# Weights' buffers at 96 instead of 64 bytes, modulo 512, above the activation slots

## Chip, cores and metric

One core of one Trainium2 chip runs the whole program. The metric is device time in microseconds (us) of one execution; lower is better. The engines are TensorE (PE, with its weight loads shown as PEld), VectorE (DVE), ScalarE (ACT), GpSimd (POOL) and the queue of SyncE (SP), which issues the transfers. SBUF is the on-chip memory, with 128 partitions; an address here is a byte offset within a partition, the same in all 128.

## What is computed

Two blocks of two transformer layers each, on 256 tokens of width 1024, in float32. Cut to its order:

```
x = first_block(x, mem, ...)     # layer 0: gated 31-wide causal convolution + memory attention
                                 # layer 1: forgetting attention + memory attention
                                 # each followed by a projection and a convolved FFN (2 x 2816 wide)
x = second_block(x, p, ...)      # retention (4 heads) + per-layer embedding,
                                 # sparse attention (16 heads; compressed, selected, window) + embedding
...
logits = einsum("bqhd,bkhd->bhqk", qb, kb) * scale + cum_logf[q] - cum_logf[k]
u = causal_dwconv(h @ w_up, w_dw, b_dw); gate, val = split(u, 2)
return (silu(gate) * val) @ w_down
```

Nearly all of the arithmetic is activations (1024 or 2816 by 256 tokens) times weight matrices, some 180 MB of weights read once.

## The kernel before

Activations are kept with channels on partitions and the 256 tokens along the partition. The weights stream from memory in one fixed order as units of 128 x 1024 float32 (512 KB), `ws[i]`, each with eight chunks of 128 x 128. `load` (SP) brings a unit into one of four `raw` buffers, some units ahead of use; `advance` (line 483 on) splits it: ACT rounds it to fp32r into `whi` (line 501), DVE or POOL subtracts to get the rest into `wlo` (line 505). There are six `whi` and six `wlo` buffers in turn. The early stages (to about 123 us: embeddings, gated convolution, memory keys) take their units unsplit, as plain float32 (`NATIVE`, tiles `wf`).

Activations that feed a split matmul lie in slots: 45 tiles of 128 x 512 fp32r, the first 256 columns the rounded half, `hi`, the others the rest, `lo` (`Split`). 38 slots are in the pool `const`; 7 more (`LATE`) are added in a pool of their own when the phase `ffn0` begins, behind a tile `gap` that nothing reads. A product of split operands is three matmuls, `mm3`, with the first argument as the stationary operand (the weight load) and the second as the moving one:

```python
    def mm3(ps, ahi, alo, bhi, blo, start, stop):
        pe.matmul(ps, lhsT=ahi, rhs=bhi, start=start, stop=False)
        pe.matmul(ps, lhsT=ahi, rhs=blo, start=False, stop=False)
        pe.matmul(ps, lhsT=alo, rhs=bhi, start=False, stop=stop)
```

These are lines 554 to 556. `proj` calls it with a weight chunk as the stationary operand and a slot's half as the moving one (one output tile of 128 channels by 256 tokens per eight or more chunks). `proj_tm` (lines 585 to 587) has the roles changed: a slot's 128 tokens are stationary, up to 512 columns of weights move. Attention logits and values have slots on both sides. Results go to PSUM tiles `acc`, `s`, `pt` or `o`, whose names stand ahead of the arrow in the rows; behind it stands the moving operand and then the stationary one. Line 572 is `proj` with unsplit weights. `conv31` (lines 859 to 868) applies 31 taps to a tile `vp` at starts that go up by one column (4 bytes): 5 taps on PE, 10 or 11 on ACT (line 865), the rest on DVE (line 868).

The order of the work on each engine is the program's own order, laid out by the tile framework, which also sets the waits. Each pool gets one stretch of a partition, in the order in which pools are opened: `const`, `wraw` (the `raw` tiles), `wspl` (`whi`, `wlo`, `wf`), `fp`, `tiny`, then the phase's pool, or from `ffn0` on the late slots and after them the phase's pool. Tiles begin at multiples of 32 bytes. In the program before, all slots, the late ones too, begin at 256 modulo 512; `raw`, `whi`, `wlo`, `wf` and the tiles of `fp` begin at 320 modulo 512. `epsc` (line 549) lies in `const` behind the slots and takes 32 bytes; the late pool's `gap` takes 64.

Of the kernel before, what the change touches and what calls it, by code (L numbers as in the profile page):

```python
# [18 lines left out]
F32 = mybir.dt.float32  # L19
# [5 lines left out]
P = 128  # L25
# [367 lines left out]
def block_kernel(ctx, tc, A, out, WL, PL, CL, SL, stop=None, dbg=None):  # L393
# [3 lines left out]
    const = ctx.enter_context(tc.tile_pool(name="const", bufs=1))  # L397
# [3 lines left out]
    tiny = ctx.enter_context(tc.tile_pool(name="tiny", bufs=4))  # L401
    dram = ctx.enter_context(tc.tile_pool(name="dram", bufs=1, space=bass.MemoryType.DRAM))
    psum = ctx.enter_context(tc.tile_pool(name="psum", bufs=1, space=bass.MemoryType.PSUM))

    rmk, r1k, rr, r3k = (const.tile([P, 2], F32, name=n) for n in ("rmk", "r1k", "rr", "r3k"))
    slots = Slots(const, NSLOTS - LATE)

# [28 lines left out]
    def phase(nm):  # L436

        phases.close()
        if nm == "ffn0":
            lp = late.enter_context(tc.tile_pool(name="late", bufs=1))  # L440
            lp.tile([P, 16], F32, name="gap")
            slots.add(lp, LATE)
        cur[0] = phases.enter_context(tc.tile_pool(name=nm, bufs=1))

# [101 lines left out]
    pool.memset(ones, 1.0)  # L546
    mhalf = const.tile([P, 2], F32, name="mhalf")
    pool.memset(mhalf, -0.5)
    epsc = const.tile([P, 2], F32, name="epsc")
    pool.memset(epsc, 1e-6)  # L550


# [137 lines left out]


    phase("conv")
    def token_stats(t, junk, ss, tt):

# [306 lines left out]

    def ffn(l, X, st, gains, stats):
        phase(f"ffn{l}")
        rb = None
        h = []
# [63 lines left out]
    def small(nm):  # L1069
# [6 lines left out]
        return hi, lo  # L1076

    phase("fox")
    wf = small("f")

# [766 lines left out]
```

## Time and profile before

| | |
|---|---|
| median of 3 runs | 1190.87 us (1187.84, 1190.87, 1197.31) |
| the profiled execution's own time | 1191.61 us |
| span of its profile, first to last instruction | 1189.8 us |
| granted TensorE clock, mean | 0.994 |
| busy: PE, PEld, DVE, ACT, POOL | 1152.0, 1105.0, 888.8, 727.2, 468.2 us |
| matmuls recorded on PE | 8924 |

The profile is of one execution. [...] A float32 matmul that is not a transpose is recorded as two.

### The profile page before, as it was taken

The numbers are of one execution on the slowest core, as the hardware profiler recorded it, in microseconds if no ns is written. First come the engines' busy times: TensorE is split into PE (matmuls) and PEld (weight loads), VectorE is DVE, ScalarE is ACT, GpSimd is POOL, SyncE is SP. The second block draws the span as 40 slices with busy tenths as digits, with TensorE's granted clock in tenths as the row PEclk, the third lists the DMA queues.
The fourth block names the chain that finished last, engine by engine and source line by source line (L and its number), as shares of the span: only waits on it lengthen the run. The fifth ranks groups of instructions, "written<-read, shape, count | busy, mean of one in ns | idle before, by whom it ended". The sixth has DMA issues, their size and how long they took to land.

```text
span 1189.8 us, 23453 instructions
## 1 busy us (share of the span) xinstructions
PE 1152.0 (97%) x8924; PEld 1105.0 (93%) x8924; DVE 888.8 (75%) x1610; ACT 727.2 (61%) x1355; POOL 468.2 (39%) x576
## 2 busy tenths in 40 slices
PE   7999999999999999999999999999999999999996
PEld 6887999999989999999999999999998799989896
DVE  1896799985669979988556867756976678988654
ACT  3755667765567666766554554546766666666554
POOL 3872624322424255332343232214464743332241
PEclk9999999999999999999999999999999999999998
DMA  9821445666544344565554555555557653333350
GB/s 354 310 99 68 164 169 202 214 195 197 191 143 142 125 136 175 195 194 189 198 181 170 187 169 185 185 171 196 178 174 263 231 188 107 125 106 116 111 174 36
DMA packets 59872, 205.61 MB, mean 173 GB/s; under 512 B 6640, under 2 KB 9072, under 8 KB 59760
## 3 DMA queue, kind: packets, MB, share of 16 engines
q1 hardware_dynamic: 59760, 204.12, 50.0%
q8 instruction: 70, 1.15, 0.4%
q14 instruction: 42, 0.34, 0.1%
HBM read 202.00 MB, written 2.10 MB: 172 GB/s over the span
## 4 chain that ended last, share of the span: by engine, by line
PE 83%; DVE 7%; ACT 4%; POOL 3%; issue 2%; DMA 1%; DVEq 0%; ACTq 0%; POOLq 0%
PE acc L555 12%; PE acc L554 12%; PE acc L556 12%; PE s L554 5%; PE s L555 5%; PE s L556 5%; PE pt L555 5%; PE pt L554 5%; PE pt L556 5%; PE acc L572 4%; PE pt L675 2%; ACT whi L501 2%; PE pt L572 2%; POOL wlo L505 2%; DVE wlo L505 1%
## 5 line engine op out<-in xcount | busy, mean ns | idle before, releaser
L501 ACT CAST whi<-raw 128x1024 fp32r<-128x1024 f32 x341 | 356.5, 1050 | 242.2 <-PE acc L555 89.1
L505 POOL TENSOR_TENSOR wlo<-raw,whi 128x256 fp32r<-128x256 f32 x384 | 320.2, 865 | 452.3 <-ACT whi L501 393.0
L505 DVE TENSOR_TENSOR wlo<-raw,whi 128x1024 fp32r<-128x1024 f32 x245 | 317.6, 1298 | 126.9 <-ACT whi L501 125.2
L555 PE MATMUL acc<-slot,whi 128*128 128x256 f32 x1336 | 373.5, 281 | 2.1 <-DVE slot L605 2.0
L554 PE MATMUL acc<-slot,whi 128*128 128x256 f32 x1336 | 370.5, 280 | 2.9 <-ACT slot L590 1.4
L556 PE MATMUL acc<-slot,wlo 128*128 128x256 f32 x1336 | 372.8, 280 | 0.0
L554 PEld LDWEIGHTS acc<-slot,whi 128*128 128x128 f32 x1336 | 251.0, 189 | 5.6 <-ACT slot L590 1.9
L555 PEld LDWEIGHTS acc<-slot,whi 128*128 128x128 f32 x1336 | 251.9, 189 | 4.2 <-DVE slot L605 2.7
L556 PEld LDWEIGHTS acc<-slot,wlo 128*128 128x128 f32 x1336 | 251.9, 189 | 0.7
L554 PE MATMUL pt<-slot,whi 128*128 128x256 f32 x508 | 141.7, 279 | 0.6 <-DVE xall L678 0.6
L555 PE MATMUL pt<-slot,whi 128*128 128x256 f32 x508 | 141.4, 278 | 0.0
L556 PE MATMUL pt<-slot,wlo 128*128 128x256 f32 x508 | 141.3, 278 | 0.0
L554 PE MATMUL s<-slot,whi 128*128 128x256 f32 x492 | 137.4, 281 | 2.7 <-DVE ca L1018 2.7
L555 PE MATMUL s<-slot,whi 128*128 128x256 f32 x492 | 137.5, 280 | 0.0
L556 PE MATMUL s<-slot,wlo 128*128 128x256 f32 x492 | 137.1, 281 | 0.0
L620 POOL TENSOR_TENSOR sqa<-sqa,sq 128x256 f32<-128x256 f32 x54 | 58.0, 1078 | 108.6 <-ACT sq L624 107.5
L554 PEld LDWEIGHTS pt<-slot,whi 128*128 128x128 f32 x508 | 96.1, 189 | 0.9 <-DVE xall L678 0.8
L554 PEld LDWEIGHTS s<-slot,whi 128*128 128x128 f32 x492 | 93.1, 190 | 3.1 <-issue 2.9
L556 PEld LDWEIGHTS pt<-slot,wlo 128*128 128x128 f32 x508 | 95.5, 188 | 0.0
L555 PEld LDWEIGHTS pt<-slot,whi 128*128 128x128 f32 x508 | 95.4, 188 | 0.1
L555 PEld LDWEIGHTS s<-slot,whi 128*128 128x128 f32 x492 | 93.1, 189 | 0.2 <-DVE slot L591 0.2
L556 PEld LDWEIGHTS s<-slot,wlo 128*128 128x128 f32 x492 | 92.9, 189 | 0.3
(391 smaller groups left out, 2048.3 us busy)
## 6 DMA issues: line engine op xcount, KB each, us to landing
raw<-ws SPq DMA_DIRECT2D x341, 512.0 KB, 3.6
wf<-ws SPq DMA_DIRECT2D x28, 512.0 KB, 7.8
xall<-xtok SPq DMA_DIRECT2D x2, 512.0 KB, 3.7
tok<-mtok SPq DMA_DIRECT2D x2, 512.0 KB, 10.2
mem<-memt SPq DMA_DIRECT2D x8, 128.0 KB, 6.8
emb<-em SPq DMA_DIRECT2D x4, 256.0 KB, 4.6
xall<-xt SPq DMA_DIRECT2D x4, 256.0 KB, 4.4
dm<-decay SPq DMA_DIRECT2D x4, 256.0 KB, 4.1
```

The costliest lines, as they stand in the source:

```text
L501: act.copy(whi[i], raw[i])
L505: eng.tensor_tensor(wlo[i][:, c:c + w], raw[i][:, c:c + w], f32(whi[i][:, c:c + w]), op=OP.subtract)
L554: pe.matmul(ps, lhsT=ahi, rhs=bhi, start=start, stop=False)
L555: pe.matmul(ps, lhsT=ahi, rhs=blo, start=False, stop=False)
L556: pe.matmul(ps, lhsT=alo, rhs=bhi, start=False, stop=stop)
L572: pe.matmul(ps, lhsT=hi, rhs=s, start=start and k == 0, stop=stop and k == len(X) - 1)
L620: pool.tensor_tensor(self.acc, self.acc, self.last, op=OP.add)
L675: pe.transpose(o, i, ident)
```

## The change

`epsc` gets 10 columns instead of 2, so that it takes 64 bytes instead of 32, and everything behind it in `const`, and each pool behind `const`, moves up by 32 bytes. The `gap` ahead of the late slots gets 8 columns instead of 16, 32 bytes instead of 64, so that the late slots stay at 256 modulo 512. `raw`, `whi`, `wlo`, `wf` and the `fp` tiles then begin at 352 modulo 512: 96 instead of 64 bytes above the slots. Only columns 0 and 1 of `epsc` are used. No other line differs.

```diff
         if nm == "ffn0":
             lp = late.enter_context(tc.tile_pool(name="late", bufs=1))
-            lp.tile([P, 16], F32, name="gap")
+            lp.tile([P, 8], F32, name="gap")
             slots.add(lp, LATE)
...
     pool.memset(mhalf, -0.5)
-    epsc = const.tile([P, 2], F32, name="epsc")
+
+    epsc = const.tile([P, 10], F32, name="epsc")
     pool.memset(epsc, 1e-6)
```

## Rows read from the trace of the kernel before

**Rows 1.** The page, busy us, share of the span and instructions.

```profile
PE 1152.0 (97%) x8924; PEld 1105.0 (93%) x8924; DVE 888.8 (75%) x1610; ACT 727.2 (61%) x1355; POOL 468.2 (39%) x576
```

**Rows 2.** The page, chain that ended last, share of the span by engine.

```profile
PE 83%; DVE 7%; ACT 4%; POOL 3%; issue 2%; DMA 1%; DVEq 0%; ACTq 0%; POOLq 0%
```

**Rows 3.** Groups of instructions by form, PE: count | busy us, mean ns | idle before.

```profile
L555 PE MATMUL acc<-slot,whi 128*128 128x256 f32 x1336 | 373.5, 281 | 2.1 <-DVE slot L605 2.0
...
L554 PE MATMUL pt<-slot,whi 128*128 128x256 f32 x508 | 141.7, 279 | 0.6 <-DVE xall L678 0.6
...
L555 PE MATMUL s<-slot,whi 128*128 128x256 f32 x492 | 137.5, 280 | 0.0
...
L586 PE MATMUL acc<-wlo,slot 128*128 128x512 f32 x80 | 31.6, 394 | 0.0
```

**Rows 4.** Stretches: start:end, length, busy (count): PE, PEld, DVE, ACT, POOL, clock, DMA.

```profile
215.00:275.00 60.00, 60.00 (x532) 60.00 (x531) 50.36 (x83) 39.56 (x65) 15.53 (x21) 1.00 0.62 203
...
497.50:557.50 60.00, 60.00 (x511) 60.00 (x511) 51.31 (x90) 42.51 (x69) 21.83 (x28) 1.00 0.59 189
```

**Rows 5.** Groups on PE, first from 200 to 260, then 505 to 565 us.

```profile
L554 PE MATMUL acc<-slot,whi 128*128 128x256 f32 x72 | 19.9, 276 | 0.0
...
L554 PE MATMUL acc<-slot,whi 128*128 128x256 f32 x74 | 20.8, 281 | 0.0
```

**Rows 6.** Timeline of PE: start us, length us; operands both slots, ten starts apart.

```profile
692.92 0.28 PE L555 MATMUL s<-slot,slot 128*128 128x256 f32 x1
...
694.12 0.28 PE L556 MATMUL s<-slot,slot 128*128 128x256 f32 x1
```

**Rows 7.** Chain that ended last, in order of time: start us, us, what.

```profile
29.84 2.16 PE s L859 x10
```

**Rows 8.** Timeline of PEld near 917 us, moving operands of 60 columns, four starts apart.

```profile
916.85 0.19 PEld L556 LDWEIGHTS s<-slot,slot 128*128 128x128 f32 x1
...
917.29 0.19 PEld L1465 LDWEIGHTS o<-whi,slot 128*122 128x122 f32 x1
```

**Rows 9.** Stretches as in rows 4, from 123 us to the end.

```profile
123.00:325.00 202.00, 201.80 (x1775) 201.40 (x1774) 161.12 (x261) 131.24 (x217) 76.54 (x87) 1.00 0.58 193
330.00:455.00 125.00, 122.06 (x950) 116.53 (x949) 99.39 (x201) 82.67 (x181) 53.64 (x68) 1.00 0.41 140
455.60:474.80 19.20, 19.20 (x166) 19.20 (x165) 19.20 (x34) 14.08 (x25) 8.28 (x9) 1.00 0.43 160
...
497.30:629.80 132.50, 132.50 (x1127) 132.50 (x1126) 93.56 (x142) 81.76 (x126) 46.76 (x56) 1.00 0.59 193
...
694.20:701.70 7.50, 7.50 (x62) 7.33 (x61) 5.37 (x8) 3.36 (x5) 0.00 (x0) 1.00 0.66 232
...
836.10:851.90 15.80, 15.80 (x136) 15.80 (x135) 14.91 (x27) 13.55 (x28) 7.63 (x9) 1.00 0.54 184
852.00:960.00 108.00, 101.51 (x751) 93.64 (x751) 78.73 (x119) 72.11 (x118) 64.77 (x74) 1.00 0.64 222
960.00:1122.00 162.00, 157.70 (x1229) 150.20 (x1228) 133.82 (x319) 97.48 (x242) 52.59 (x68) 0.99 0.33 114
...
1158.40:1178.00 19.60, 19.60 (x168) 19.60 (x167) 10.83 (x23) 11.82 (x25) 5.33 (x8) 1.00 0.00 1
```

**Rows 10.** Timeline of PE, token-major projection (proj_tm), seven starts apart.

```profile
682.73 0.39 PE L586 MATMUL acc<-wlo,slot 128*128 128x512 f32 x1
...
684.33 0.39 PE L587 MATMUL acc<-whi,slot 128*128 128x512 f32 x1
```

**Rows 11.** Instructions on tile vp: duration ns min/median/max, first and last start, forms.

```profile
L868 DVE SCALAR_TENSOR_TENSOR s<-vp,par,s x92: 464/490/491, 32.0 to 89.8; 128x256 f32<-128x256 f32 x92
...
L859 PE MATMUL s<-vp,wf x60: 377/378/380, 29.7 to 77.6; 128*128 128x256 f32 x60
L865 ACT ACTIVATE cvt<-vp,par x58: 492/508/513, 24.9 to 79.3; 128x256 f32<-128x256 f32 x58
```

**Rows 12.** DMA issues by line: count, KB each, median us to landing.

```profile
raw<-ws SPq DMA_DIRECT2D x341, 512.0 KB, 3.6
```

## Prediction

> **What bounds the kernel now.** I read the page first. TensorE (PE) is busy 97% of the span [rows 1], and the chain that ended last lies 83% on PE [rows 2]. So the time is a count of matmuls times the beat at which they follow each other. The largest kind is the 128x256 fp32r matmul with a weight chunk as the stationary operand and a half slot as the moving one: 3 x (1336 + 508 + 492) = 7008 of PE's 8924 records [rows 1, 3]. All of them have one address relation, since chunks step by 512 bytes and half slots by 1024: weights stand 64 bytes above the activations, modulo 512. The change makes that 96.
>
> The next view is a table of stretches in which PE never idles. From 215 to 275 us PE ran 532 matmuls in 60 us, from 497.5 to 557.5 us only 511 [rows 4]. Two matmuls at the edges overlap a window, so the beats are 60/530 = 113.2 ns and 60/509 = 117.9 ns. [...] A matmul's mean duration tells them apart too, 276 ns in one and 281 ns in the other [rows 5]. I call them the short and the long beat; from 497.3 to 629.8 us the long one is 132.5/1125 = 117.8 ns [rows 9]. I take 113.3 and 117.8, a difference of 4.45 ns, which agrees with 281 - 276. A stretch keeps its beat for up to 200 us and changes it only after an interruption.
>
> That the relation of the addresses has a part in it is seen where both operands are slots, that is at 0 bytes: there ten matmuls took 694.12 - 692.92 = 1.20 us, 120 ns each [rows 6]. [...] A plausible reading is that the stream of the moving operand and the load of the next weights collide in SBUF, and that it matters where in their course they meet.
>
> **The change part by part.** The widened epsc is 32 bytes more in the constants' pool behind the slots. It pushes raw, whi, wlo, the fp tiles and the conv tiles up by 32 bytes. The gap ahead of the seven late slots shrinks by the same 32, so these slots and all tiles of the later phases stay where they were. No instruction, semaphore or transfer is added, removed or moved; a memset of 10 columns in place of 2 lies on GpSimd in the first microseconds and is nothing.
>
> Cost on the 7008 matmuls: unknown, since no row shows a long run at 96 bytes. The nearest rows bound it. From below: at best the beat is that of weight loads alone. With a moving operand of 60 columns, four weight loads followed each other in 917.29 - 916.85 = 0.44 us [rows 8], 110 ns with an error of 2 or 3; say 111.7, 1.6 ns under the short beat. From above: 120 ns, as at 0 bytes. Between them lie the two beats that exist at 64 bytes.
>
> The value that I take is the short beat everywhere. 0 bytes, where the two streams start at the same place, has the worst beat; 64 bytes has a good and a bad one; the farther the start is from 0, the less a small shift after an interruption should bring them together. It is an extrapolation from two points, and I treat it as one.
>
> The sum. The stretches that stand at the long beat and in which PE does not wait are 455.6 to 474.8 (166 matmuls), 497.3 to 629.8 (1127), 836.1 to 851.9 (136), 1158.4 to 1178.0 (168), and three like 694.2 to 701.7 (62 each, one per retention head) [rows 9]. Less two each for the edges: 164 + 1125 + 134 + 166 + 3 x 60 = 1769 matmuls, times 4.45 ns = 7.9 us, all on the path. The stretch 123 to 325 us (1775) is at the short beat and gives nothing. In the rest, some 7008 - 1769 - 1775 = 3460 matmuls, beats alternate. If half were long, as in the two sets above, that would be 1730 x 4.45 = 7.7 us; but there PE waits (2.9 us of idle time from 330 to 455, 6.5 from 852 to 960, 4.3 from 960 to 1122 [rows 9]), the beat restarts after every wait, and a wait swallows what PE saves ahead of it. Ends 0 and 7.7; I take 1.5. Sum 9.4 us.
>
> What hides behind PE and could come out: from 497.5 to 557.5 us VectorE is busy 51.31 of 60 us [rows 4], which becomes 51.31/57.7 = 89% at the short beat and still fits. From 455.6 to 474.8 it is busy all of the 19.2 us [rows 9]; there the 164 x 4.45 = 0.7 us may come back as a wait for VectorE, which the low end of the mixed stretches covers. Weights are prefetched over four units ahead, and a 512 KB unit lands in 3.6 us [rows 12], so 4% more demand on DMA at a share of 0.59 [rows 4] doesn't bind.
>
> The token-major projections have the roles changed: a slot is stationary and 512 columns of whi are moving, at -64 bytes, hereafter -96. [...] There are 3 x 80 of them [rows 3], so their whole excess is 240 x 13 ns = 3 us; I leave it at 0, with ends of -3 and +3. Matmuls between slots don't change.
>
> Engines that read tiles at a new place: the tap operands of the 31-wide convolution start at every multiple of 4 bytes, and ScalarE took 492 to 513 ns, VectorE 464 to 491, PE 377 to 380 for all of them [rows 11]. So I cost 32 bytes at nothing on these engines.
>
> The profiled execution took 1191.6 us with a span of 1189.8, 0.7 above the median of 1190.87. 1191.6 - 9.4 - 0.7 = 1181.5; I say 1181. The scatter of the three runs, 1187.84 to 1197.31, is what different draws of the beats would give; so less than 1%, 12 us, can hardly be told from no change.
>
> **The rivals.** (1) Tighter than the short beat. If 96 bytes free the two streams of each other, the beat goes to 111.7: 7008 x 1.6 = 11.2 us more, 1170. [...] Against it: a beat that holds for 200 us (1775 matmuls from 123 to 325 us [rows 9]) looks like a bound of its own, and back-to-back weight loads are close to it.
>
> (2) Nothing changes: both beats exist at 96 as at 64, with another draw. 1190, and 1186 to 1197 by the draw. [...]
>
> (3) Slower. 0 and 64 are whole multiples of 64 bytes, 96 is not. If PE fetches in blocks of 64 bytes, every 512-byte weight chunk now touches nine blocks in place of eight. [...] 7008 x 6.7 = 47 us less the long-beat share that has already paid (1769 x 4.45 = 8 and some of the mixed), so at most +35, 1226; if only the long beat becomes the rule, (7008 - 1769 - 800) x 4.45 = 20 us, less what waits swallow, 1206. It decides from the first fp32r matmul at 123 us. For it: all long runs that I can read stand on multiples of 64. Against it: plain fp32 passes at odd places pay nothing [rows 11].
>
> (4) The padding does not arrive: the allocator packs in steps of 32 bytes, so 40 bytes could only fail to move the pools if epsc's room was there already. Its neighbours stand 32 bytes apart, so I give it no chance of its own; it would look like (2).
>
> **How the numbers follow.** Short beat everywhere 0.42, at 1181 (1176 to 1186, by the mixed stretches and the token-major ones); tighter 0.20, at 1170 (1163 to 1176); unchanged 0.15, at 1190; slower 0.23, from 1200 to 1226. The predicted time is the first case's. The range runs from 1170, which leaves out half of the tighter case, 0.10, to 1212, which leaves out somewhat under half of the slower one, 0.10. Faster by over 1% means under 1179: the tighter case and a third of the first, 0.34. Slower by over 1%, over 1203: 0.21 of the slower case's 0.23. The rest, 0.45, is within 1%.
>
> **What would show it.** In the changed profile the table of stretches should count 529 to 532 matmuls in any 60 us without idle time, 497 to 630 us as well as 215 to 275, and mean durations of 276 ns in both; the slot-by-slot rows should stay at 120. If counts of 511 persist in some stretches, it is (2); if 502 or fewer stand everywhere, (3); if over 535, (1). I am wrong altogether if the beats are unchanged and the time moves all the same: then another engine or the transfers felt the 32 bytes. Beats that depend on more than this relation, on the moment of the restart for one, would make the extrapolation worthless.

## The result and the profile after

| | before | after |
|---|---|---|
| median, 4 runs each | 1190.25 us (1187.84 to 1197.31) | 1206.64 us (1205.35 to 1207.95) |
| the profiled execution | 1191.61 us | 1207.89 us |
| its span | 1189.8 us | 1206.1 us |

The ratio is 1.0123, with a 95% interval of 1.0091 to 1.0155: slower by 16 us where 9 us of gain were forecast. The time lies within the range, the sign is wrong.

The page after, first the busy times, then the shares of the chain that ended last, as in [rows 1, 2]:

```profile
PE 1169.4 (97%) x8924; PEld 1122.3 (93%) x8924; DVE 887.8 (74%) x1610; ACT 727.2 (60%) x1355; POOL 464.3 (38%) x576
...
PE 82%; DVE 7%; ACT 3%; DMA 3%; POOL 2%; issue 2%; SPq 0%; DVEq 0%; ACTq 0%; POOLq 0%
```

The counts are those of before. Busy time counts overlapping records once: in [rows 6] a matmul's record is 0.28 us long and starts follow each other after 0.12 us. PE's busy time grew by 1169.4 - 1152.0 = 17.4 us, the span by 16.3. VectorE, ScalarE and POOL are busy as long as before to within 4 us. So nobody else became the bound, and no transfer did: PE works longer on the same instructions. The groups by form, as in [rows 3]:

```profile
L555 PE MATMUL acc<-slot,whi 128*128 128x256 f32 x1336 | 375.5, 282 | 2.1 <-DVE slot L605 2.0
...
L554 PE MATMUL pt<-slot,whi 128*128 128x256 f32 x508 | 142.7, 281 | 0.4 <-DVE xall L678 0.4
...
L555 PE MATMUL s<-slot,whi 128*128 128x256 f32 x492 | 138.0, 281 | 0.1
...
L586 PE MATMUL acc<-wlo,slot 128*128 128x512 f32 x80 | 31.8, 397 | 0.0
```

A mean duration grows by 1 to 3 ns, and the idle time behind the bar stays. How often one matmul follows the other is seen in the table of stretches, which answers to [rows 4, 9]; the columns are start:end, length, busy and count of PE, PEld, DVE, ACT, POOL, granted clock, DMA share, GB/s:

```profile
123.00:325.00 202.00, 202.00 (x1719) 201.81 (x1718) 157.15 (x257) 127.58 (x212) 70.52 (x79) 1.00 0.56 188
215.00:275.00 60.00, 60.00 (x514) 60.00 (x513) 49.86 (x82) 38.75 (x65) 14.04 (x19) 1.00 0.58 189
...
464.20:483.30 19.10, 19.10 (x165) 19.10 (x164) 19.10 (x34) 14.08 (x25) 8.36 (x9) 1.00 0.43 160
502.00:634.00 132.00, 132.00 (x1115) 132.00 (x1114) 94.48 (x148) 84.30 (x131) 47.75 (x58) 1.00 0.60 195
```

With two matmuls off for the edges, 215 to 275 us is 60/512 = 117.2 ns (before 113.2), and 502 to 634 us is 132/1113 = 118.6 ns (before 117.8). Counted from the starts of the matmuls in a stretch, the two values are 117.3 and 118.7. The short beat of before is found in no stretch. The granted clock is 1.00 in all of them, as in [rows 4]. The groups of the same stretches as in [rows 5], 200 to 260 and 505 to 565 us, no longer differ by 5 ns:

```profile
L554 PE MATMUL acc<-slot,whi 128*128 128x256 f32 x72 | 20.1, 280 | 0.0
...
L554 PE MATMUL acc<-slot,whi 128*128 128x256 f32 x72 | 20.2, 281 | 0.0
```

What the change did not touch stayed. Slot by slot, at 0 bytes, ten starts still take 703.32 - 702.12 = 1.20 us, as in [rows 6]. In the token-major projection, where the roles are changed, two starts that are 17 matmuls apart lie 694.89 - 690.93 = 3.96 us from each other, 233 ns each against 229 in [rows 10]. From the timeline of PE, start us and length us:

```profile
690.93 0.39 PE L585 MATMUL acc<-whi,slot 128*128 128x512 f32 x1
...
694.89 0.39 PE L587 MATMUL acc<-whi,slot 128*128 128x512 f32 x1
...
702.12 0.28 PE L554 MATMUL s<-slot,slot 128*128 128x256 f32 x1
...
703.32 0.28 PE L555 MATMUL s<-slot,slot 128*128 128x256 f32 x1
```

Where the 16.3 us lie: the 1773 matmuls that had the short beat from 123 to 325 us need 1773 x 202/1717 = 208.6 us, 6.6 more. The 1125 that had the long beat from 497 us on need 1125 x 0.8 ns = 0.9 us more. The 240 token-major ones add 240 x 4 ns = 1.0. The remaining 7.8 us are left, by difference, to the other 4100 matmuls, 1.9 ns each, which had a mixture of both beats. So the loss falls on one kind of matmul: 3.7 ns where it had the short beat, 0.8 where it had the long one.

### The profile page after: what moved, and what is told of

It is laid out like the page before. It is cut to its first block, busy times and chain, and to the rows that moved or that the text cites. A ratio compares the mean times of both kernels' runs of the same rounds, so it can differ in the third digit from the quotient of the medians.

```text
span 1206.1 us, 23453 instructions
## 1 busy us (share of the span) xinstructions
PE 1169.4 (97%) x8924; PEld 1122.3 (93%) x8924; DVE 887.8 (74%) x1610; ACT 727.2 (60%) x1355; POOL 464.3 (38%) x576
## 4 chain that ended last, share of the span: by engine, by line
PE 82%; DVE 7%; ACT 3%; DMA 3%; POOL 2%; issue 2%; SPq 0%; DVEq 0%; ACTq 0%; POOLq 0%
PE acc L555 12%; PE acc L554 12%; PE acc L556 12%; PE s L554 5%; PE s L555 5%; PE s L556 5%; PE pt L555 4%; PE pt L554 4%; PE pt L556 4%; PE acc L572 4%; DMA raw<-ws 3%; PE pt L675 2%; POOL wlo L504 2%; PE pt L572 2%; ACT whi L500 2%
## 5 line engine op out<-in xcount | busy, mean ns | idle before, releaser
L504 POOL TENSOR_TENSOR wlo<-raw,whi 128x256 fp32r<-128x256 f32 x384 | 315.6, 854 | 467.7 <-ACT whi L500 412.6
```

The source lines that it names most:

```text
L504: eng.tensor_tensor(wlo[i][:, c:c + w], raw[i][:, c:c + w], f32(whi[i][:, c:c + w]), op=OP.subtract)
```

## Experiments

The theory at this point, a reading of the beats that no trace shows: two streams of PE, the moving operand and the next weights, collide in SBUF, and the distance of their addresses decides how much. Rivals: the weights' own start (352, no multiple of 64, the block rival of the prediction), a chance draw of the beats, or something behind PE. "Beat" is from here on the mean time from start to start of 128x256 weight matmuls over 30 or more in an undisturbed stretch. A distance is that of the weights above the slots, modulo 512 bytes.

**Relation or place.** Both operands moved by 32 bytes, the distance stays at 64:

```diff
+    const.tile([P, 8], F32, name="front")
     slots = Slots(const, NSLOTS - LATE)
```

> Slots and weights both start 32 bytes higher than before (288 and 352 modulo 512), so they are 64 bytes apart as before, while the weights stand where the changed kernel has them. If the relation of the two addresses alone sets the beat: 113.3 and 117.8 ns as before, about 1190 us. If it is the weights' own start at 32 modulo 64, the block rival of the prediction: no stretch at 113.3, 117.3 to 118.7 ns throughout, about 1206 us.

1197.09 us (1187.0 to 1203.16), ratio 1.003 (0.9989 to 1.007). The weights start at 352 modulo 512 as in the changed kernel, and the beats are those of before, only in other stretches:

```profile
200.00:260.00 60.00, 60.00 (x512) 60.00 (x511) 50.80 (x85) 39.89 (x67) 15.67 (x20) 1.00 0.63 196
515.00:575.00 60.00, 60.00 (x532) 60.00 (x531) 52.07 (x86) 43.25 (x69) 20.03 (x28) 1.00 0.63 199
```

512 matmuls in 60 us are the long beat, 117.8 ns, 532 the short one, 113.3, and here it is the early stretch that has the long one. So the weights' start is not the cause. The counterpart has the same front tile, and the change on top (`epsc` of 10 columns, `gap` of 8): slots at 288, weights at 384, a multiple of 64, distance 96.

> Slots 32 bytes and weights 64 bytes higher than before (288 and 384), 96 bytes apart, with the weights on a multiple of 64. Relation alone: 117.3 and 118.7 ns, about 1206 us, as the changed kernel. Weights' own start alone: 113.3 and 117.8 ns, about 1190 us.

1208.67 us, ratio 1.0126 (1.0085 to 1.0166), the changed kernel's loss and its beats:

```profile
200.00:260.00 60.00, 60.00 (x514) 60.00 (x513) 51.59 (x87) 39.56 (x67) 15.74 (x20) 1.00 0.66 200
515.00:575.00 60.00, 60.00 (x508) 60.00 (x507) 49.66 (x84) 41.34 (x66) 18.57 (x24) 1.00 0.64 190
```

The distance of 96 costs the 16 us; neither place does.

**The draw.** The kernel before once more, with nothing changed but a comment.

> The kernel before, unchanged, profiled once more. If the beat of a stretch is drawn anew at each execution: 113.3 and 117.8 ns again, but in other stretches than before (123 to 325 us need not be at 113.3, 497 to 630 us not at 117.8). If the program sets it: the same beats in the same stretches. Time 1187 to 1203 us either way.

1197.95 us, and the same two beats in other stretches than in its first profile:

```profile
200.00:260.00 60.00, 60.00 (x512) 60.00 (x511) 51.33 (x87) 38.94 (x66) 15.71 (x20) 1.00 0.61 195
515.00:575.00 60.00, 60.00 (x532) 60.00 (x531) 52.13 (x88) 43.27 (x69) 19.69 (x26) 1.00 0.62 195
```

In [rows 4] the early stretch had the short beat and the late one the long. So at 64 bytes the program alone does not settle which of its two beats a long stretch has. It is not chance throughout: of 70 stretches of 20 or more intervals without a wait, 51 had the same beat in both profiles. The 19 that changed, the two longest among them, hold 3800 of their 6130 intervals. The mean beat is 115.1 ns in the first profile and 115.7 in this one, which makes 7008 x 0.6 = 4 of the 6.3 us between the two executions; the other 2 us were not followed up. In all rounds the kernel before took 1186.94 to 1205.57 us, 1188.77 to 1205.57 on one chip alone. The four executions of the changed one, whose two beats are 1.4 ns apart, took 1205.35 to 1207.95. The draw fits that scatter; with two of these executions profiled it is shown only in part.

**Other distances.** The same two tiles, other sizes; where `epsc` and `gap` together would not fit, `onesT` goes from `const` to the phase's pool:

```diff
-            lp.tile([P, 16], F32, name="gap")
+            lp.tile([P, g], F32, name="gap")
...
-    epsc = const.tile([P, 2], F32, name="epsc")
+    epsc = const.tile([P, e], F32, name="epsc")
...
-    onesT = const.tile([FR, T], F32, name="onesT")
+    onesT = cur[0].tile([FR, T], F32, name="onesT")
```

(e, g) is (122, 24) for 32 bytes, (18, none) for 128, (26, 120) for 160, (34, 112) for 192, (42, 104) for 224, (50, 96) for 256 and (98, 48) for 448, that is -64.

> Weights 32 bytes above the slots; the tile onesT moves into the phase's pool to make room. If an odd multiple of 32 is what costs: no stretch at 113.3, about 1206 us, and the same two beats as at 96 bytes. If nearness to 0 is what costs: 120 ns as at 0 bytes in most stretches, about 1220 us.

> Weights 128 bytes above the slots, both on multiples of 64; the gap tile is left out. If distances of whole multiples of 64 keep the short beat: 113.3 ns in long stretches again, 1180 to 1195 us. If the beat grows with the distance from 64: 118 ns or more everywhere, over 1206 us.

> Weights 256 bytes above the slots; onesT moved. If the pattern repeats every 256 bytes: 120 ns as at 0 bytes, 1215 to 1225 us. If every 512: something between 113 and 120 ns; the farthest point from a collision at the start, it would then be the best place if the short beat were a matter of clearance.

> Weights 64 bytes below the slots (448 above, modulo 512); onesT moved to make room. If the sign does not matter: 113.3 and 117.8 ns, 1187 to 1203 us. If what counts is how far the weights are ahead: no 113.3, over 1205 us.

> Weights 192 bytes above the slots; onesT moved. If the pattern repeats every 256 bytes, 192 is -64: 113.3 and 117.8 ns. If it repeats every 512 only and distance costs, 118.7 ns or more, over 1205 us.

> Weights 160 bytes above the slots, -96 in a pattern that repeats every 256; onesT moved. If the sign does not matter: 117.3 and 118.7 ns as at 96, 1205 to 1212 us. If it does: another beat; only a place with the short beat alone, 113.3, would beat the kernel before, at about 1181 us.

> Weights 224 bytes above the slots, -32 in a pattern that repeats every 256; onesT moved. If the sign does not matter: 118.3 ns as at 32, about 1209 us; otherwise another beat.

| distance | us | before, same chip | matmuls in 60 us from 250, from 515 us | beat, ns |
|---|---|---|---|---|
| 32 | 1209.19 | 1191.63 | 510, 510 | 118.2 to 118.3 |
| 128 | 1212.55 | 1191.63 | 508, 508 | 118.7, in some stretches 120.0 |
| 160 | 1218.43 | 1198.93 | 503, 502 | 120.0 |
| 192 | 1201.89 | 1197.59 | 511, 512 | 117.8, in pieces 113.3 |
| 224 | 1200.40 | 1198.93 | 517, 517 | 116.7, in some stretches 117.8 |
| 256 | 1215.03 | 1197.59 | 503, 502 | 120.0 |
| 448 | 1205.95 | 1197.59 | 511, 511 | 117.8, in pieces 113.3 |

The times at 32 and 128 bytes are medians of 4 runs (ratios 1.0124 and 1.0159, intervals 1.0078 to 1.017 and 1.0116 to 1.0202), the others one run each. Two lines of the table, the late stretch at 160 and at 256 bytes:

```profile
515.00:575.00 60.00, 60.00 (x502) 60.00 (x501) 49.99 (x87) 42.15 (x69) 18.88 (x25) 1.00 0.61 192
...
515.00:575.00 60.00, 60.00 (x502) 60.00 (x502) 50.03 (x87) 41.67 (x68) 18.45 (x24) 1.00 0.60 193
```

256 bytes have 120.0 ns as 0 bytes have, and 192 and 448 have 117.8 ns both, with their short pieces in the same three places (near 705, 743 and 781 us): in these two pairs the pattern repeats after 256 bytes. "The farther from 0, the better" is refuted: 160 bytes, far from 0 and from 256, are as bad as these, 120.0 ns.

**Is it a collision of the two streams?** The changed kernel, with one operand of `proj` held still: its first column is read 128 or 256 times, with step 0, so that products are other numbers. First the weights, then the moving operand.

```diff
+            hi, lo = (t[:, 0:1].broadcast_to([P, P]) for t in (hi, lo))
```

> The changed kernel (96 bytes) with the weight chunk of each projection read as its first column 128 times (step 0); the products are other numbers, the count, order and start addresses of the instructions are the same. If two moving streams that meet in SBUF set the beat, a weight load that stays at one address meets the activations otherwise: the 117.3 and 118.7 ns vanish, and the beat falls to 113.3 or the 111.7 of bare weight loads, 1165 to 1185 us. If the price hangs on the start addresses alone (a block more at the start of each operand): 117.3 and 118.7 ns stay, about 1206 us.

```diff
-            mm3(ps, hi, lo, s.hi, s.lo, start and k == 0, stop and k == len(X) - 1)
+            mh, ml = (t[:, 0:1].broadcast_to([P, 256]) for t in (s.hi, s.lo))
+            mm3(ps, hi, lo, mh, ml, start and k == 0, stop and k == len(X) - 1)
```

> The changed kernel (96 bytes) with the moving operand of each projection read as its first column 256 times (step 0); again other numbers, the same instructions and starts. Two streams that meet: the beat falls to 113.3 or less, 1165 to 1185 us. Start addresses alone: 117.3 and 118.7 ns stay, about 1206 us.

1188.53 and 1175.20 us, one run each, with 1198.93 for the kernel before on the same chip. The first lies above the 1165 to 1185 that were expected. A stretch at the short beat and one at 120 ns (20/167) in the first:

```profile
160.00:320.00 160.00, 160.00 (x1414) 160.00 (x1414) 130.36 (x217) 104.43 (x170) 50.04 (x57) 1.00 0.61 195
...
1155.00:1175.00 20.00, 20.00 (x169) 20.00 (x168) 10.83 (x23) 11.77 (x25) 5.34 (x8) 1.00 0.00 1
```

The stretches of the second:

```profile
200.00:260.00 60.00, 60.00 (x540) 60.00 (x539) 53.27 (x92) 42.83 (x72) 20.63 (x24) 1.00 0.64 209
515.00:575.00 60.00, 60.00 (x539) 60.00 (x539) 48.13 (x76) 40.80 (x62) 14.83 (x20) 1.00 0.68 209
```

With a moving operand that stays at one address the beat is 111.7 ns in nearly every stretch, the value that the prediction had put at the floor from weight loads alone [rows 8]. With still weights 113.3 holds for some three quarters of the matmuls; 17% stand at 116.7 and 9% at 120.0. So the loss of 96 bytes is gone when the moving operand stands still, and for the most part when the weights do. Start addresses alone, which are the same in all three kernels, can't explain that: the price hangs on the walk of both streams. Whether a step of 0 is read in some other way than a walk was not set apart.

**Finer distances, in bursts.** A small program of nothing but bursts of 40 matmuls of that shape, six bursts for each distance, after different waits; it computes nothing of the reference.

> A program that computes none of the reference: bursts of 40 fp32r matmuls of the kernel's form, six bursts at each distance of weights above activations, every 16 bytes from 0 to 240 and every 4 bytes around 64, some bursts after another matmul, some after a wait. If the short beat belongs to whole multiples of 64 bytes: 113.3 ns occurs at 64 and 192 alone and is gone at 60 and 68. If it belongs to a stretch of distances around 64: 113.3 also at 48 to 80, and one of them may have it alone. If the streams' courses count and nothing else: 0, 128 and 160 at 118.7 to 120, as in the full kernel.

Beats of the last thirty matmuls of a burst, in ns, by distance, bursts at a lower granted clock left out (the execution's mean is 0.984): 0: 120.0; 16 and 32: 118.2 to 118.4; 48: 117.7 to 117.8; 52: 113.3 in five of six; 56: 117.7 to 117.9; 60: 119.2 to 119.6; 64: 113.3 or 117.8; 68 and 72: 118.2 to 118.3; 76: 113.3 in all six; 80: 118.7; 84: 119.9 to 120; 96: 117.3 or 118.7; 112: 119.8 to 120; 128: 120.0 in three of five, 118.7 in two; 144 and 160: 120; 176: 118.0 to 118.2; 192: 117.8; 208: 116.7; 224: 116.6 or 117.8; 240: 120.1, in two of six 117.5. The bursts repeat what the whole kernel showed at 32, 64, 96, 160 and 224 bytes. At 192 they show its main beat only, at 128 more of the 120.0 that it had in some stretches. The short beat sits at isolated places 12 bytes apart, 52, 64 and 76, with worse ones 4 bytes beside them. 76 bytes seemed to have it alone, which called for the whole kernel at 76.

**76 bytes in the whole kernel.** Tiles begin at multiples of 32 bytes, so the slots were made views into one tile, 20 bytes into it; the tile is 32 bytes longer, which moves the weights to 352. The control starts 32 bytes into it, distance 64.

```diff
-        self.free += [pool.tile([P, 512], F32R, name=f"slot{i}") for i in range(self.n, self.n + n)]
+        big = pool.tile([P, 512 * n + 8], F32R, name=f"slots{self.n}")
+        self.free += [big[:, 5 + 512 * i:517 + 512 * i] for i in range(n)]
...
-            lp.tile([P, 16], F32, name="gap")
+            lp.tile([P, 8], F32, name="gap")
```

> The 76-byte distance in the whole kernel: the slots are views into one tile and start 20 bytes into it, so that the weights lie 76 bytes, modulo 512, above them; order and waits of the instructions are those of the kernel before. Theory (the distance of the two operands sets the beat, and 76 bytes has the short one alone, as the bursts had it): 113.3 ns in every stretch of weight matmuls. The kernel before had a mean interval of 115.1 ns over some 6750 weight matmuls; 1.8 ns each are 12 us, less what waits take in, so 1181 us (1176 to 1186), ratio 0.985 to 0.996 against the kernel before. Rival (the bursts had only one pair of buffers each, and the kernel, with its many, draws as before): beats of 113.3 and 117.8, 1187 to 1203 us. Rival (slots that start off the 32-byte grid cost the engines that write and read them): VectorE's busy time goes above 890 us and the time does not fall though the beat does.

> Control: the same single tile, but the slots start 32 bytes into it, so the weights lie 64 bytes above them as in the kernel before. Theory: two beats, 113.3 and 117.8 ns, drawn by the stretch; 1187 to 1203 us, ratio 0.995 to 1.008 against the kernel before. Were it the single tile that gains and not the distance, this kernel would be as fast as its sibling at 76 bytes, about 1181 us.

A plain miss for the first: 1230.44 us (1227.17 to 1233.68), ratio 1.0266 (1.0227 to 1.0306), the slowest kernel of all. The control: 1195.19, ratio 0.9977 (0.9943 to 1.001), beats 113.3 and 117.8; so the single tile is not to blame. The stretches at 76 bytes:

```profile
250.00:310.00 60.00, 60.00 (x502) 60.00 (x501) 40.48 (x60) 33.82 (x53) 15.21 (x20) 1.00 0.58 183
515.00:575.00 60.00, 60.00 (x489) 60.00 (x488) 48.10 (x84) 39.98 (x65) 20.74 (x28) 1.00 0.58 182
```

60/500 = 120.0 and 60/487 = 123.2 ns, the second above everything so far. VectorE's busy time, 886.8 us, is no higher, so the rival of the slower engines falls too. One thing that differs from the bursts: there the moving operand started on the 32-byte grid and the weights 12 bytes off it, here the moving operand is off it. The last three kernels set these apart.

**Which of the two is off the grid.** Bursts again, for pairs of the moving operand's start and the distance.

> Computes nothing of the reference: the bursts again, six of 40 matmuls for each of 26 pairs of (start of the moving operand, distance of the weights above it), in bytes. Theory (a moving operand that starts off the 32-byte grid costs more): 113.3 ns at 0/76 and at 32/76, about 119.5 at 20/76 as in one76, and more than at 0/64 at 20/64. Rival (only the distance counts): 113.3 at 76 bytes for every start. Second rival (bursts and kernel differ otherwise): 0/76 and 20/76 alike, and w76 as slow as one76. Distance 332 as 76 if the pattern repeats after 256 bytes. At 40, 88 and 100 bytes 113.3 ns would show the steps of 12 bytes going on.

Beats by start/distance, bursts at a lower granted clock left out (the execution's mean is 0.991): 0/76: 113.3 in five of six, once 120.0; 32/76: 113.3; **20/76: 123.3**; 4/76: 121.1; 8/76: 120.1; 12/76: 118.4; 16/76: 119.9 to 120.1; 0/64: 113.3 or 117.8; 16/64 and 32/64: 113.3; 8/64: 120.9; 20/64: 118.3; 0/52: 113.3, once 120.1; 12/52: 117.8; 20/52: 121.5 to 121.7; 0/96: 117.3 or 118.7; 32/96: 118.7; 20/96: 123.3; 0/88: 113.3 or 116.7; 0/40: 119.2; 0/44: 117.8; 0/84 and 0/100: 120; 0/92: 118.1 to 118.5; 0/108: 122.3 in three of five, 120.0 in two; 0/332: 113.3. The table of stretches for 20/76, 32/76 and 16/64, each over five or six bursts without a break:

```profile
66.00:94.00 28.00, 28.00 (x229) 28.00 (x229) 0.57 (x4) 3.93 (x10) 0.00 (x0) 1.00 0.00 1
...
210.00:236.00 26.00, 26.00 (x232) 26.00 (x231) 0.57 (x4) 3.93 (x10) 0.00 (x0) 1.00 0.00 1
330.00:356.00 26.00, 26.00 (x232) 26.00 (x231) 0.57 (x4) 3.94 (x10) 0.00 (x0) 1.00 0.00 1
```

28/227 = 123.3 against 26/230 = 113.0 at the same distance: the start counts beside the distance. No pair whose moving operand starts 4, 8, 12 or 20 bytes off reached 113.3. Nor are weights off the grid harmless at every distance: 0/108 has the moving operand on it and went to 122.3. The 120.0 that most stretches of the whole kernel with its slots at 76 bytes had did not occur in the bursts at 20/76. 332 goes as 76 does, 256 less. The steps of 12 bytes end at 52 and 88: 40 and 100 are bad.

**The weights off the grid instead.** The slots stay, the twelve weight buffers become views 12 bytes into one tile. The plain fp32 weights share these buffers and had to come through POOL's queue, rounded.

```diff
+    wone = wspl.tile([P, 2 * WBUFS * UNIT + 8], F32R, name="wone")
...
+    def wbuf(tag):
+        o = 3 + UNIT * (wat[tag] % WBUFS + (0 if tag == "whi" else WBUFS))
...
-            whi[i] = wspl.tile([P, UNIT], F32R, tag="whi", name=f"whi{i}")
+            whi[i] = wbuf("whi")
...
+            if i in WL.native:
+                nc.gpsimd.dma_start(raw[i], ws[i].bitcast(F32R))
```

The control starts at 0 in place of 3 columns, distance 64.

> The weights instead of the slots off the grid: the slots lie where they lay, the twelve buffers of the weights are views into one tile that start 12 bytes into it, 76 bytes, modulo 512, above the slots. The weights that stay plain fp32 share these buffers and come in through POOL's queue, rounded, which changes some products slightly and the first 200 us in time. Theory (the distance sets the beat, and at 76 bytes it depends on which of the two starts off the 32-byte grid; the moving operand off it costs more): 113.3 ns in the stretches of weight matmuls after 200 us, about 1180 us if the first 200 us stay, less than its sibling by 8 to 14 us. Rival (the bursts' 113.3 ns at 76 bytes holds only for one pair of buffers): 119 to 120 ns as in one76, about 1230 us.

> Control for w76: the same views, the same queue for the plain weights, start at 0 bytes, so 64 bytes above the slots as in the kernel before. Both theories: two beats, 113.3 and 117.8 ns, by the stretch; 1187 to 1203 us and what POOL's queue costs in the first 200 us.

1195.07 us (1191.46 to 1196.76) and 1204.69 (1200.95 to 1205.83) on the same chip: 9.6 us less at 76 bytes, and the ranges don't touch. The stretches of the kernel at 76 bytes, both at the short beat, and of the control:

```profile
200.00:260.00 60.00, 60.00 (x532) 60.00 (x531) 54.90 (x96) 43.26 (x73) 20.24 (x24) 1.00 0.68 215
515.00:575.00 60.00, 60.00 (x532) 60.00 (x531) 53.33 (x90) 42.09 (x70) 21.24 (x27) 1.00 0.66 205
```

```profile
200.00:260.00 60.00, 60.00 (x512) 60.00 (x511) 52.28 (x91) 41.45 (x70) 18.89 (x24) 1.00 0.66 203
515.00:575.00 60.00, 60.00 (x512) 60.00 (x511) 51.37 (x91) 42.84 (x70) 22.07 (x28) 1.00 0.64 195
```

At 76 bytes the stretch from 136 to 161 us had 120.0 and ten short ones later, of 22 to 36 matmuls, as well, together 8% of the matmuls; the others had 113.3. Here too, then, there are two beats, as once in six bursts at 0/76. Against the kernel before it is 1.002 (0.9997 to 1.0043): what the beat gains is lost at the start. The waits of the control's first 140 us show where, engine, line waited for, us in total, times, longest:

```profile
PE s L582 <- DMA sq<-pt: 10.0, 1, 10.0
```

The kernel at 76 bytes has the same wait with 9.6 us, the kernel before has none of it, and the first weight matmuls come 10 us later than before in both. The transfer that is waited for is not one of the plain weights'; that their new queue holds it up is likely, not shown. Without that wait 1195.07 - 9.6 = 1185 us could be expected, an estimate, 6 us below the 1191.39 of the kernel before on that chip. Such a kernel was not tried, and none that was measured and computes the same beats the kernel before.

## Why the prediction was wrong

**What held.** PE bounds the kernel, and the 128x256 weight matmuls' beat sets the time. Over the profiled executions the mean beat of all of them (intervals over 130 ns, which hold a wait, left out) and the time go together: 115.1 ns and 1191.6 us before, 117.9 and 1207.9 after, 121.3 and 1230.6 for the slots at 76 bytes, 111.7 and 1175.2 for the still moving operand. That is 4.8 to 6.3 us for each ns of the beat, somewhat less than 7 for 7008 matmuls, as if waits took in a part, as the prediction said. Smaller differences follow the beat less closely, as the repeated profile showed. No instruction or transfer was added or moved. The ends of the beat's range, 111.7 and 120, held in these runs where both operands start on the 32-byte grid; 122.3 was seen with the weights alone off it, 123.3 with the moving operand off it.

**The step that failed** is "The value that I take is the short beat everywhere", with its reason "the farther the start is from 0, the less a small shift after an interruption should bring them together". It was an extrapolation from two points, and the curve is nothing that two points could tell: over one period of 256 bytes the beat goes 120.0 (0), 118.2 (32), 113.3 or 117.8 (64), 117.3 or 118.7 (96), 118.7 (128), 120.0 (160), 113.3 or 117.8 (192), 116.7 or 117.8 (224). 64 was one of the few places that have the short beat at all, and nearly every step away from it loses. In the changed kernel no stretch had the short beat, 117.3 and 118.7 ns stood in its place, and a gain of 9.4 us became a loss of 16. The 9.4 us are the price of the long beat in the kernel before, and of the right order: the kernel whose weights lie at 76 bytes gained 9.6 us on its control, whose own draws differ by the run, and by the estimate above 6 us on the kernel before. The term was given to the wrong distance. That the range holds the time at all is owed to the room that it left for the slower rival, not to the mechanism that was forecast.

Three readings are slightly off, and none matters. The stretches like 694.2 to 701.7 us take 7.5/60 = 125 ns in the mean and hold only 48 matmuls at the long beat, not 60, 0.2 us less for the three. The stretch from 123 to 325 us is not one run of the short beat: 32 matmuls from 150.9 to 154.6 us have the long one. Nor did the beat change only after an interruption: at 439.0 us of the same profile it goes from 117.8 to 113.3 ns over an interval of 124 ns, without idle time.

**The rivals.** (1) The tighter beat, 111.7, exists, but only when the moving operand stands still; no distance that was measured gave it. (2) That beats are drawn was right for 64 bytes (the repeated profile), and its 1190 us wrong, since at 96 the drawn beats are others. The distance is worth something: at a granted clock of 1.00 the beat was 113.3 or 117.8 ns at 64 bytes, 117.3 or 118.7 at 96 and 120.0 at 160, and 111.7 at 96 when the moving operand stands still. (3) Slower came true, with the time of its milder case, "only the long beat becomes the rule", 1206 against 1206.64 measured. The size fits because both beats at 96 bytes lie around the long one, 117.8; that the rival has the number is luck, for its mechanism, blocks of 64 bytes that the weights straddle, is refuted: with weights at 352 and slots at 288 the beats of before came back, 113.3 and 117.8 ns, with weights at 384, a multiple of 64, the loss stayed, at 1208.67 us. No run shows the 6.7 ns of its larger case as the price of one more block; measured are 120 ns at 0 bytes [rows 6] and 113.3 for the short beat. (4) The padding arrived. Of the counts that the prediction named as signs, none came: 514 and 508 matmuls in 60 us are neither 529 to 532, nor 511, nor 502, nor over 535.

**The last paragraph** of the prediction had the right reserve, "beats that depend on more than this relation": the draw at each interruption and the moving operand's own start are such things. The token-major term, taken at 0 with ends of 3 us, came to 1.0. No run shows the 13 ns of excess that those ends are made of; measured are 229 ns per matmul before and 233 after.

**What stays open.** Why the good distances lie where they do, 12 bytes apart and then no more, what decides the draw at a restart, and why a moving operand off the grid costs up to 10 ns (113.3 at 0/76, 123.3 at 20/76). No run looked inside SBUF. Shown is that the distance makes the loss and that it takes the walk of both streams (117.3 and 118.7 ns at 96 bytes, 111.7 with the moving operand still, 113.3 for the most part with the weights still); that they collide in SBUF is the reading that fits, and no run here shows the collision itself.

## What to carry to other kernels

In this kernel, whose fp32r matmuls each load new weights, the distance of the two operands' buffers was a tuning knob worth some per cent (medians from 1190 to 1230 us, the start of the moving operand included). In another one it is to be measured, with a burst of matmuls per distance and per start, because here a value said nothing of those between it and the next: 113.3 or 117.8 ns at 64 bytes, 118.2 to 118.3 at 68 and 72, 113.3 at 76. When stretches of the same work differ in their beat, and not in the same way in each execution, compare beats stretch by stretch in a profile: one time can't tell a draw from a change. A small program's finding is to be carried over with all of its conditions; here the moving operand's start was one that nobody had listed.

## What was not expected of the hardware

The beat of one instruction at a granted clock of 1.00 had at least ten values between 111.7 and 123.3 ns, most of them steady to 0.1 or 0.2 ns over a stretch. The pattern of distances repeats after 256 bytes in the three pairs that were measured (0 and 256 with 120.0 ns, 192 and 448 with 117.8 and pieces of 113.3, 76 and 332 with 113.3). Four bytes decide: 113.3 ns at 76 bytes, 118.7 at 80. At the same distance of 76 bytes, 20 bytes of shift of both operands raise the beat from 113.3 to 123.3 ns, 32 bytes don't. At 64 bytes a stretch took one of two beats within its first 15 matmuls or so and kept it, with one exception in the first profile (at 439.0 us), for up to 177 us (155.8 to 333.2 us in the repeated profile, 1507 matmuls at 117.8).
